# The first projection's opening: the squares' matmul placed amid the modulation row, X*rstd right behind it, one weight tile loaded first, and one later modulation pair held back

## The chip, the cores and the metric

The kernel runs on one core of a Trainium2 chip. Times are device microseconds (us), from the start of the program on the core to its end. The engines are TensorE (PE, with its weight loads shown apart as PEld), VectorE (DVE), ScalarE (ACT), GpSimd (POOL) and SyncE (SP), which here issues the DMAs. Each engine works through its own queue in order; semaphores join them.

## The reference, cut to what matters

Two transformer-like blocks follow each other on 512 tokens of width 1024, in fp32. The change touches the opening of the first one:

```python
mod = silu(c) @ w_ada + b_ada                       # 6 * 1024 values, one row
shift1, scale1, gate1, shift2, scale2, gate2 = split(mod, 6)
h = rms_norm(x, norm1_w) * (1 + scale1) + shift1    # rms_norm: x * rsqrt(mean(x*x) + eps) * w
proj = h @ w_in                                     # q, k, v, z, alpha, beta, ... of the delta rule and attention
...
qkv = silu(causal_dwconv(concat(q, k, v)))          # 4 taps; then the gated delta rule, in chunks of 64
...
x = x + gate1 * (mix @ w_o)                         # gate1, shift2, scale2, gate2 are used from here on
```

## The kernel before, in words

Activations lie transposed: 128 channels on the partitions, 512 tokens along the free axis, eight tiles k = 0 to 7 for the width of 1024. `X0` is x, `H[0]` and `H[1]` are the high and the low part of h (each weight and each activation is split in two, and `mm3` adds three matmuls, lines 314 to 316, so a projection tile of 128 outputs is 24 matmuls of 512 columns).

*The opening* (lines 395 to 481). 18 warm-up matmuls on zeros run while the first DMAs land. SP loads the vectors, x in two halves, the constants, four tiles of `w_ada1` (512 KB each), then `cb`, the row c spread over 128 partitions, and from there twelve tiles of `w_adaT` and five weight tiles in turn. The modulation is made in two ways. scale1's first half is a row on PE: `row_ps`, four tiles q with two fp32 matmuls each (two passes a matmul in the trace), which is copied to SBUF by ACT and turned into columns by the small `adcol` matmuls; with it comes `s1[:, 0:4]`. The other twelve columns (shift1, and scale1 for k of 4 and more) are products on DVE, `on_dve`: a tile of `w_adaT` times Silu of `cb`, summed along the free axis. The norm is: squares on ACT, sums on DVE (`acc`), one fp32 matmul with ones (`ss`), then Ln and Exp on ACT (`rstd`). For each k follow X*rstd on DVE, scale and shift on ACT (line 472), the split into H on ACT and DVE, and for k below 5 the load and split of one of the first five weight tiles (`first_w`, tiles 8, 9, misc, 0, 1). The first projection then is 120 matmuls over k and these five tiles.

*The delta stage* (from line 484). Stages t = 0 to 5 are lists of steps that `merge` interleaves by a position between 0 and 1: projections with their convolution (`conv_silu`: one ACT scaling out of PSUM and three DVE operations of line 560 that read the same PSUM tile, then Silu), the preparation of head pairs (`pre_steps`: E, sums, `kk`, which writes 16 small blocks to `scr` in HBM, then the substitution, which reads them back), the chain over chunks, and steps of the second modulation. For t = 0 the list has weight tiles 16 and 17; for t = 1 tile 10 is the first. Projections write into two PSUM buffers (`PSM`) from there on.

*The second modulation* (`ada_steps`, lines 331 to 352) makes 32 more columns of `mod`, which are first used after the delta stage. Its own `cb` is loaded and put through Silu when `ada_steps` is called, ahead of the lists. Each step one(j) loads four half tiles (`adraw`, two buffers) and does four products on DVE (line 344). No step of it stands in the list of t = 0; two stand in that of t = 1, at the positions 0.125 and 0.375. The projection of tile 10 is at 0.083 there, the two halves of `kk` at 0.121 and 0.170, the read back at 0.219.

*What sets the order.* The order in which lines are written is not the order in which an engine runs them. A planner goes through the program with a cost model and gives each engine, whenever it is free, the earliest written instruction whose inputs and buffers it takes to be ready. `tc.keep_in_program_order(i)` puts instruction i behind the one written before it on the same engine; what is written after i is not bound by it. ACT's functions come in table sets: `actf` (lines 248 to 267) loads the set with Ln and Exp by hand, ahead of the first of them and behind the activations of other sets that `acts` has noted in `before`; other loads are placed where a function needs them.

Of the kernel before, what the change touches and what calls it, by code (L numbers as in the profile page):

```python
# [8 lines left out]
F32 = mybir.dt.float32  # L9
F32R = mybir.dt.float32r  # L10
I32 = mybir.dt.int32
AF = mybir.ActivationFunctionType
# [3 lines left out]
P = 128  # L16
T = 512
# [195 lines left out]
def _body(ctx, tc, A):  # L213
# [20 lines left out]
    def C(name, i=0, n=None):  # L234
        o, m = CO[name]
        t = DC[0] if name in DNAMES else CS
        return t[:, o + i:o + (m if n is None else i + n)]
# [15 lines left out]
    def actf(func, **kw):  # L253
        if func not in (AF.Ln, AF.Exp):
            i = nc.scalar.activation(func=func, **kw)
            after(i, group)
            before.append(i)
            table[0] = None
            return i
        if table[0] is None:  # L260
            table[0] = tc.keep_in_program_order(nc.scalar.preload_act_table_set("natural_log_exp_and_others"))
            after(table[0], before)
            before.clear()
            group.clear()
        i = nc.scalar.activation(func=func, **kw)
        after(i, [table[0]])
        group.append(i)
        return i

    def acts(func, **kw):  # L270
        i = nc.scalar.activation(func=func, **kw)
        before.append(i)
        table[0] = None
        return i
# [23 lines left out]
    def wload(src, kt, n, own=None):  # L298
        sp = SP[0]
        if own is None:  # L300
            raw = sp.tile([P, CH], F32, tag="raw", name="raw", bufs=2)
            hi = sp.tile([P, CH], F32R, tag="hi", name="hi")
            lo = sp.tile([P, CH], F32R, tag="lo", name="lo")
        else:
            raw = own.tile([P, CH], F32, tag="ad", name="praw", bufs=15)
            hi = own.tile([P, CH], F32R, tag="phi", name="phi", bufs=len(FIRST))
            lo = own.tile([P, CH], F32R, tag="plo", name="plo", bufs=len(FIRST))
        m = kt * n
        nc.sync.dma_start(out=raw[:, :m].rearrange("p (k c) -> p k c", k=kt), in_=src)
        split(raw[:, :m], hi[:, :m], lo[:, :m])  # L310
        return (hi[:, :m].rearrange("p (k c) -> p k c", k=kt), lo[:, :m].rearrange("p (k c) -> p k c", k=kt))
# [18 lines left out]

    def ada_steps(pl):
        cb = pl.tile([P, D], F32, name="cb")
        nc.sync.dma_start(out=cb, in_=A["crow"].to_broadcast([P, D]))
        acts(func=AF.Silu, out=cb, in_=cb)

        def one(j):
            if j % 4 == 0:
                st["am"] = pl.tile([P, 4, 2], F32, tag="am", name="am", bufs=2)
            for jj in (j, j + 1):
                for q in range(2):  # L340
                    raw = pl.tile([P, T], F32, tag="adraw", name="adraw", bufs=2)
                    qs = slice(q * T, q * T + T)
                    nc.sync.dma_start(out=raw, in_=A["w_adaT"][12 + jj][:, qs])
                    nc.vector.tensor_tensor_reduce(out=raw, in0=raw, in1=cb[:, qs], scale=1.0, scalar=0.0,
                                                   op0=ALU.mult, op1=ALU.add, accum_out=st["am"][:, jj % 4, q:q + 1])
            if j % 4 == 2:
                o = mod[:, 14 + j:18 + j]
                nc.vector.tensor_tensor(out=o, in0=st["am"][:, :, 0], in1=st["am"][:, :, 1], op=ALU.add)
                nc.vector.tensor_tensor(out=o, in0=o, in1=V("b_ada", 14 + j, 4), op=ALU.add)

        st = {}
        return [lambda j=j: one(j) for j in range(0, 32, 2)]
# [42 lines left out]
    with pool("w0", 1) as w0:  # L395
# [13 lines left out]
        def ad_tile():  # L409
            return w0.tile([P, D], F32, tag="ad", name="ad", bufs=15)  # L410

        row_ps = pst.tile([P, T], F32, tag="st", name="adrow")
        for q in range(4):
            raw = ad_tile().rearrange("p (k c) -> p k c", k=2)
            nc.sync.dma_start(out=raw, in_=A["w_ada1"][q])
            for k in range(2):
                nc.tensor.matmul(row_ps[0:1], csil[:, 2 * q + k:2 * q + k + 1], raw[:, k],
                                 start=(q + k == 0), stop=(q == 3 and k == 1))
        row = w0.tile([1, T], F32, name="adrow0")
        nc.scalar.activation(out=row, in_=row_ps[0:1], func=AF.Copy)  # L420
        colp = pz.tile([P, T], F32, tag="z", name="adcol")
# [10 lines left out]
            nc.vector.tensor_tensor_reduce(out=raw, in0=raw, in1=cb, scale=1.0, scalar=0.0,  # L432
                                           op0=ALU.mult, op1=ALU.add, accum_out=am[:, m:m + 1])

        def sadd(out, a, b):
            nc.vector.tensor_tensor(out=out, in0=a, in1=b, op=ALU.add)

        acc = w0.tile([P, T], F32, name="acc0")
        for k in range(KD):
            sq = acc if k == 0 else w0.tile([P, T], F32, tag="sq", name="sq", bufs=2)  # L440
            nc.scalar.activation(out=sq, in_=X0[:, k], func=AF.Square)
            if k:
                sadd(acc, acc, sq)
        ss = ppre.tile([P, T], F32, tag="pre", name="ssx")
        nc.tensor.matmul(ss, C("ones"), acc, start=True, stop=True)
        rstd = w0.tile([P, T], F32, name="rstd")
        actf(AF.Ln, out=rstd, in_=ss, scale=1.0 / D, bias=eps)
        actf(AF.Exp, out=rstd, in_=rstd, scale=-0.5)

        W0 = {}  # L450

        def first_w(i):
            if i == "misc":
                W0[i] = wload(A["w_misc"], KD, 80, w0)
            else:
                W0[i] = wload(A["w_dn"][i], KD, P, w0)
            PS0[i] = (PSM[0] if i in FIRST[:2] else pfirst).tile([P, T], F32, tag="mm", name="mm")

        sadd(mod[:, 8:12], colp[:, 0:4], V("b_ada", 8, 4))
        nc.vector.scalar_tensor_tensor(out=s1[:, 0:4], in0=mod[:, 8:12], scalar=1.0, in1=V("norm1_w", 0, 4),  # L460
                                       op0=ALU.add, op1=ALU.mult)
        order = {0: 8, 1: 9, 2: "misc", 3: 0, 4: 1}
        for k in range(KD):
            if k >= 4:
                on_dve(4 + k, 8 + k)
                sadd(mod[:, 8 + k:9 + k], am[:, 8 + k:9 + k], V("b_ada", 8 + k))
                nc.vector.scalar_tensor_tensor(out=s1[:, k:k + 1], in0=mod[:, 8 + k:9 + k], scalar=1.0,
                                               in1=V("norm1_w", k), op0=ALU.add, op1=ALU.mult)
            on_dve(k, k)
            sadd(mod[:, k:k + 1], am[:, k:k + 1], V("b_ada", k))  # L470
            nc.vector.tensor_tensor(out=X0[:, k], in0=X0[:, k], in1=rstd, op=ALU.mult)
            nc.scalar.activation(out=X0[:, k], in_=X0[:, k], func=AF.Identity, scale=s1[:, k:k + 1],
                                 bias=mod[:, k:k + 1])
            split(X0[:, k], H[0][:, k], H[1][:, k])
            if k < len(FIRST):
                first_w(order[k])
        for k in range(KD):
            for i in FIRST:
                o = PS0[i][:80] if i == "misc" else PS0[i]
# [1297 lines left out]
```

## Time and profile before

| | |
|---|---|
| Median of three runs | 2149.95 us (2148.91 to 2151.90) |
| The profiled execution's own time | 2146.85 us |
| Its span on the core | 2145.0 us |
| Mean granted TensorE clock | 0.994 of 2.4 GHz |
| PE busy | 2112.7 us (98%) |
| DVE busy | 1209.2 us (56%) |
| ACT busy | 896.7 us (42%) |

The span runs from the first to the last instruction on the core; 1.85 us lie around it. All positions below are us from the span's start. The granted clock is 1.00 at 2.4 GHz and 0.50 at 1.2 GHz.

### The profile page before, as it was taken

How to read it: one execution, taken by the hardware profiler on the slowest of the kernel's cores; microseconds unless marked ns; L12 is line 12 of the kernel's file. 1: busy time of each engine (PE TensorE's matmuls, PEld its weight loads, DVE VectorE, ACT ScalarE, POOL GpSimd, SP SyncE). 2: the span in 40 equal slices, each digit the busy share in tenths (PEclk: the TensorE clock that was granted, in tenths of full speed). 3: DMA queues.
4: the chain of work that ended last, by engine and by line, in shares of the span. 5: the costliest groups of instructions: out<-in, count | busy, mean ns of one | idle time of the engine just before them, and what ended most of it. 6: DMA issues, size and time to landing. Idle time of an engine off the chain costs nothing.

```text
span 2145.0 us, 27476 instructions
## 1 busy us (share of the span) xinstructions
PE 2112.7 (98%) x10616; PEld 1718.3 (80%) x10616; DVE 1209.2 (56%) x2267; ACT 896.7 (42%) x1479; POOL 19.1 (1%) x50
## 2 busy tenths in 40 slices
PE   8999999999999999999999999999999999999997
PEld 5787877788888878888888887787888888888886
DVE  6776757565554554444335898555554554334446
ACT  5645433465553353333224323634443343223333
POOL 0000000000000000000000000000000000000000
PEclk9999999999999999999999999999999999999999
DMA  7443324222223343333333222133223433333332
GB/s 305 130 125 102 105 84 136 64 70 74 64 76 131 101 135 106 113 108 96 99 98 113 88 75 93 55 107 95 84 84 89 147 91 97 98 98 99 98 93 75
DMA packets 88682, 219.84 MB, mean 102 GB/s; under 512 B 23512, under 2 KB 28776, under 8 KB 87912
## 3 DMA queue, kind: packets, MB, share of 16 engines
q1 hardware_dynamic: 88552, 218.10, 32.8%
q8 instruction: 83, 1.36, 0.3%
q14 instruction: 47, 0.39, 0.1%
HBM read 211.50 MB, written 7.08 MB: 102 GB/s over the span
## 4 chain that ended last, share of the span: by engine, by line
PE 87%; DVE 6%; ACT 2%; SPq 2%; DMA 2%; issue 1%; DVEq 0%; ACTq 0%
PE mm L314 24%; PE mm L315 24%; PE mm L316 24%; PE pp L720 2%; DVE yc L1309 1%; DVE lo L296 1%; PE po L1082 1%; SPq L712 1%; PE tps L1246 1%; PE tps L1247 1%; PE tps L1248 1%; SPq L710 1%; PE ssp L602 1%; PE bpo L1638 1%; PE pw L793 1%
## 5 line engine op out<-in xcount | busy, mean ns | idle before, releaser
L295 ACT ACTIVATE hi<-raw 128x1024 fp32r<-128x1024 f32 (+4 forms) x349 | 346.6, 993 | 786.1 <-PE mm L315 671.3
L296 DVE TENSOR_TENSOR lo<-raw,hi 128x1024 fp32r<-128x1024 f32 (+4 forms) x349 | 397.9, 1141 | 453.5 <-ACT hi L295 443.8
L314 PE MATMUL mm<-H,hi 128*128 128x512 f32 x816 | 325.7, 399 | 5.5 <-DVE G L524 4.2
L316 PE MATMUL mm<-H,lo 128*128 128x512 f32 x816 | 324.3, 397 | 0.0
L315 PE MATMUL mm<-H,hi 128*128 128x512 f32 x816 | 324.2, 397 | 0.0
L314 PEld LDWEIGHTS mm<-H,hi 128*128 128x128 f32 x816 | 154.2, 189 | 39.7 <-ACT hi L295 4.6
L314 PE MATMUL mm<-XN,hi 128*128 128x512 f32 (+1 forms) x456 | 180.4, 396 | 0.0
L316 PEld LDWEIGHTS mm<-H,lo 128*128 128x128 f32 x816 | 154.2, 189 | 32.3 <-issue 3.0
L315 PEld LDWEIGHTS mm<-H,hi 128*128 128x128 f32 x816 | 154.2, 189 | 32.1 <-issue 3.2
L315 PE MATMUL mm<-XN,hi 128*128 128x512 f32 (+1 forms) x456 | 178.5, 391 | 0.0
L316 PE MATMUL mm<-XN,lo 128*128 128x512 f32 (+1 forms) x456 | 178.5, 391 | 0.0
L314 PEld LDWEIGHTS mm<-XN,hi 128*128 128x128 f32 (+1 forms) x456 | 85.0, 186 | 19.0 <-issue 1.0
L316 PEld LDWEIGHTS mm<-XN,lo 128*128 128x128 f32 (+1 forms) x456 | 84.9, 186 | 18.9 <-issue 0.8
L315 PE MATMUL mm<-HN,hi 128*128 128x512 f32 x256 | 100.1, 391 | 0.0
L314 PE MATMUL mm<-HN,hi 128*128 128x512 f32 x256 | 99.7, 389 | 0.0
L314 PE MATMUL mm<-F,hi 128*128 128x512 f32 x256 | 99.7, 389 | 0.0
L315 PE MATMUL mm<-F,hi 128*128 128x512 f32 x256 | 99.7, 389 | 0.0
L316 PE MATMUL mm<-HN,lo 128*128 128x512 f32 x256 | 99.7, 389 | 0.0
L316 PE MATMUL mm<-F,lo 128*128 128x512 f32 x256 | 99.7, 389 | 0.0
L315 PEld LDWEIGHTS mm<-XN,hi 128*128 128x128 f32 (+1 forms) x456 | 85.0, 186 | 17.6 <-issue 0.7
L1309 DVE SCALAR_TENSOR_TENSOR yc<-cp,cdh,yc 128x512 f32<-128x512 f32 x120 | 89.8, 750 | 2.9
L315 PE MATMUL mm<-FF,hi 128*128 128x512 f32 x176 | 68.5, 389 | 0.0
(676 smaller groups left out, 3887.4 us busy)
## 6 DMA issues: line engine op xcount, KB each, us to landing
raw<-in_w_ff SPq DMA_DIRECT2D x64, 512.0 KB, 3.6
raw<-in_ffn_up SPq DMA_DIRECT2D x44, 512.0 KB, 3.5
adraw<-in_w_adaT SPq DMA_DIRECT2D x64, 256.0 KB, 3.2
raw<-in_w_ga SPq DMA_DIRECT2D x32, 512.0 KB, 3.5
raw<-in_w_dn SPq DMA_DIRECT2D x28, 512.0 KB, 3.9
raw<-in_w_br SPq DMA_DIRECT2D x32, 256.0 KB, 2.7
raw<-in_ffn_down SPq DMA_DIRECT2D x16, 448.0 KB, 3.4
ad<-in_w_adaT SPq DMA_DIRECT2D x12, 512.0 KB, 10.2
```

Of the source, the lines that this page charges most:

```text
L295: nc.scalar.activation(out=hi, in_=src, func=AF.Copy)
L296: nc.vector.tensor_tensor(out=lo, in0=src, in1=hi.bitcast(F32), op=ALU.subtract)
L314: nc.tensor.matmul(ps, wh, xh, start=start, stop=False)
L315: nc.tensor.matmul(ps, wh, xl, start=False, stop=False)
L316: nc.tensor.matmul(ps, wl, xh, start=False, stop=stop)
L602: nc.tensor.matmul(ssp[64 * h:64 * h + 64, kind * 8 + c:kind * 8 + c + 1], sq[:, c], C("ones", 0, 1), start=True, stop=True)
L710: nc.sync.dma_start(out=U[r0:r0 + 16, :, r0:r0 + 16], in_=scr[1, q0:q0 + 4].rearrange("c j i -> j c i"))
L712: nc.sync.dma_start(out=Xb[r0:r0 + 16, :, r0:r0 + 16], in_=scr[2, q0:q0 + 4].rearrange("c j i -> j c i"))
L720: nc.tensor.matmul(pp[:, c4], lh[:, c4], rh[:, c4], start=True, stop=True)
L793: nc.tensor.matmul(pw[64 * h:64 * h + 64], st["wt"][b][:, c4, 64 * h:64 * h + 64], S[:, h], start=True, stop=True)
L1082: nc.tensor.matmul(po[:, qs], VT[:, kb, hh], pT[:, kb * P:kb * P + P], start=(kb == 0), stop=(kb == qb))
L1309: i = nc.vector.scalar_tensor_tensor(out=ycs[m], in0=cps[m][:, s:s + T], scalar=cdh[:, m * 31 + s:m * 31 + s + 1], in1=ycs[m], op0=ALU.mul ...
```

## The change

In `ada_steps`, the load of `cb` and its Silu move into the first step, one(0), and that load and the half tiles of the first column (jj = 0) are pinned behind what is written before them on SP. In the opening, squares, sums and `first_w` are written ahead of the modulation row, and the first weight tile (8) is loaded there; the `ss` matmul is pinned behind the row's second tile (q = 1), and Ln, Exp and all eight X*rstd are written right behind it. The loop over k loads the other four weight tiles, each one step of k earlier than before.

```diff
@@ -330,17 +330,20 @@
 
     def ada_steps(pl):
         cb = pl.tile([P, D], F32, name="cb")
-        nc.sync.dma_start(out=cb, in_=A["crow"].to_broadcast([P, D]))
-        acts(func=AF.Silu, out=cb, in_=cb)
 
         def one(j):
+            if j == 0:
+                tc.keep_in_program_order(nc.sync.dma_start(out=cb, in_=A["crow"].to_broadcast([P, D])))
+                acts(func=AF.Silu, out=cb, in_=cb)
             if j % 4 == 0:
                 st["am"] = pl.tile([P, 4, 2], F32, tag="am", name="am", bufs=2)
             for jj in (j, j + 1):
                 for q in range(2):
                     raw = pl.tile([P, T], F32, tag="adraw", name="adraw", bufs=2)
                     qs = slice(q * T, q * T + T)
-                    nc.sync.dma_start(out=raw, in_=A["w_adaT"][12 + jj][:, qs])
+                    i = nc.sync.dma_start(out=raw, in_=A["w_adaT"][12 + jj][:, qs])
+                    if jj == 0:
+                        tc.keep_in_program_order(i)
                     nc.vector.tensor_tensor_reduce(out=raw, in0=raw, in1=cb[:, qs], scale=1.0, scalar=0.0,
                                                    op0=ALU.mult, op1=ALU.add, accum_out=st["am"][:, jj % 4, q:q + 1])
             if j % 4 == 2:
@@ -409,6 +412,26 @@
         def ad_tile():
             return w0.tile([P, D], F32, tag="ad", name="ad", bufs=15)
 
+        def sadd(out, a, b):
+            nc.vector.tensor_tensor(out=out, in0=a, in1=b, op=ALU.add)
+
+        acc = w0.tile([P, T], F32, name="acc0")
+        for k in range(KD):
+            sq = acc if k == 0 else w0.tile([P, T], F32, tag="sq", name="sq", bufs=2)
+            nc.scalar.activation(out=sq, in_=X0[:, k], func=AF.Square)
+            if k:
+                sadd(acc, acc, sq)
+        W0 = {}
+
+        def first_w(i):
+            if i == "misc":
+                W0[i] = wload(A["w_misc"], KD, 80, w0)
+            else:
+                W0[i] = wload(A["w_dn"][i], KD, P, w0)
+            PS0[i] = (PSM[0] if i in FIRST[:2] else pfirst).tile([P, T], F32, tag="mm", name="mm")
+
+        order = {0: 8, 1: 9, 2: "misc", 3: 0, 4: 1}
+        first_w(order[0])
         row_ps = pst.tile([P, T], F32, tag="st", name="adrow")
         for q in range(4):
             raw = ad_tile().rearrange("p (k c) -> p k c", k=2)
@@ -416,6 +439,15 @@
             for k in range(2):
                 nc.tensor.matmul(row_ps[0:1], csil[:, 2 * q + k:2 * q + k + 1], raw[:, k],
                                  start=(q + k == 0), stop=(q == 3 and k == 1))
+            if q == 1:
+                ss = ppre.tile([P, T], F32, tag="pre", name="ssx")
+                tc.keep_in_program_order(nc.tensor.matmul(ss, C("ones"), acc, start=True, stop=True))
+                rstd = w0.tile([P, T], F32, name="rstd")
+                actf(AF.Ln, out=rstd, in_=ss, scale=1.0 / D, bias=eps)
+                actf(AF.Exp, out=rstd, in_=rstd, scale=-0.5)
+        
+                for k in range(KD):
+                    nc.vector.tensor_tensor(out=X0[:, k], in0=X0[:, k], in1=rstd, op=ALU.mult)
         row = w0.tile([1, T], F32, name="adrow0")
         nc.scalar.activation(out=row, in_=row_ps[0:1], func=AF.Copy)
         colp = pz.tile([P, T], F32, tag="z", name="adcol")
@@ -432,34 +464,9 @@
             nc.vector.tensor_tensor_reduce(out=raw, in0=raw, in1=cb, scale=1.0, scalar=0.0,
                                            op0=ALU.mult, op1=ALU.add, accum_out=am[:, m:m + 1])
 
-        def sadd(out, a, b):
-            nc.vector.tensor_tensor(out=out, in0=a, in1=b, op=ALU.add)
-
-        acc = w0.tile([P, T], F32, name="acc0")
-        for k in range(KD):
-            sq = acc if k == 0 else w0.tile([P, T], F32, tag="sq", name="sq", bufs=2)
-            nc.scalar.activation(out=sq, in_=X0[:, k], func=AF.Square)
-            if k:
-                sadd(acc, acc, sq)
-        ss = ppre.tile([P, T], F32, tag="pre", name="ssx")
-        nc.tensor.matmul(ss, C("ones"), acc, start=True, stop=True)
-        rstd = w0.tile([P, T], F32, name="rstd")
-        actf(AF.Ln, out=rstd, in_=ss, scale=1.0 / D, bias=eps)
-        actf(AF.Exp, out=rstd, in_=rstd, scale=-0.5)
-
-        W0 = {}
-
-        def first_w(i):
-            if i == "misc":
-                W0[i] = wload(A["w_misc"], KD, 80, w0)
-            else:
-                W0[i] = wload(A["w_dn"][i], KD, P, w0)
-            PS0[i] = (PSM[0] if i in FIRST[:2] else pfirst).tile([P, T], F32, tag="mm", name="mm")
-
         sadd(mod[:, 8:12], colp[:, 0:4], V("b_ada", 8, 4))
         nc.vector.scalar_tensor_tensor(out=s1[:, 0:4], in0=mod[:, 8:12], scalar=1.0, in1=V("norm1_w", 0, 4),
                                        op0=ALU.add, op1=ALU.mult)
-        order = {0: 8, 1: 9, 2: "misc", 3: 0, 4: 1}
         for k in range(KD):
             if k >= 4:
                 on_dve(4 + k, 8 + k)
@@ -468,12 +475,11 @@
                                                in1=V("norm1_w", k), op0=ALU.add, op1=ALU.mult)
             on_dve(k, k)
             sadd(mod[:, k:k + 1], am[:, k:k + 1], V("b_ada", k))
-            nc.vector.tensor_tensor(out=X0[:, k], in0=X0[:, k], in1=rstd, op=ALU.mult)
             nc.scalar.activation(out=X0[:, k], in_=X0[:, k], func=AF.Identity, scale=s1[:, k:k + 1],
                                  bias=mod[:, k:k + 1])
             split(X0[:, k], H[0][:, k], H[1][:, k])
-            if k < len(FIRST):
-                first_w(order[k])
+            if k < 4:
+                first_w(order[k + 1])
         for k in range(KD):
             for i in FIRST:
                 o = PS0[i][:80] if i == "misc" else PS0[i]
```

## Rows read from the trace of the kernel before

**Rows 1.** The page, whole span: busy us, share and instructions of each engine.
```profile
PE 2112.7 (98%) x10616; PEld 1718.3 (80%) x10616; DVE 1209.2 (56%) x2267; ACT 896.7 (42%) x1479; POOL 19.1 (1%) x50
```

**Rows 2.** Windows by stage: us, busy (instructions) per engine, PEclk, DMA share, GB/s.
```profile
0.00:56.15 56.15, 46.35 (x165) 30.36 (x165) 38.61 (x74) 30.70 (x42) 6.13 (x16) 0.94 0.78 303
56.15:83.00 26.85, 22.63 (x125) 18.26 (x125) 21.53 (x45) 20.03 (x31) 0.00 (x0) 0.87 0.39 115
...
104.00:160.00 56.00, 56.00 (x315) 46.30 (x312) 44.72 (x121) 26.14 (x44) 0.00 (x0) 1.00 0.40 120
```

**Rows 3.** Waits of PE from 56 to 160 us: total us, times, longest.
```profile
PE mm L314 <- DVE G L524: 4.2, 1, 4.2
```

**Rows 4.** Windows, as rows 2: granted clock (PEclk) in short stretches.
```profile
9.00:10.00 1.00, 0.00 (x0) 0.00 (x0) 0.79 (x3) 0.77 (x2) 0.00 (x0) 1.00 1.01 414
23.50:24.00 0.50, 0.00 (x0) 0.00 (x0) 0.50 (x2) 0.50 (x2) 0.00 (x0) 0.50 1.06 426
71.50:72.00 0.50, 0.00 (x0) 0.00 (x0) 0.44 (x3) 0.50 (x2) 0.00 (x0) 0.50 0.67 242
78.00:79.00 1.00, 1.00 (x6) 0.83 (x5) 0.36 (x2) 1.00 (x2) 0.00 (x0) 0.98 0.24 29
```

**Rows 5.** Timeline of PE, 0 to 26 us: start, us, instruction, idle before.
```profile
1.42 6.70 PE L405 MATMUL zero<-wz 128*128 128x512 f32 x18 [1.42 <-POOL wz L402]
10.63 7.03 PE L417 MATMUL adrow<-ad,csil 128*1 128x512 f32 x16 [2.51 <-ACT sq L441]
17.59 1.13 PE L445 MATMUL ssx<-acc,CS 128*128 128x512 f32 x2
18.80 1.05 PE L423 MATMUL adcol<-CS,adrow 1*128 1x1 f32 x8
25.26 0.79 PE L314 MATMUL mm<-H,phi 128*128 128x512 f32 x1 [5.42 <-ACT H L295]
```

**Rows 6.** Timeline of DVE, 63 to 73 us.
```profile
63.20 0.75 DVE L560 SCALAR_TENSOR_TENSOR cacc<-mm,VS,cacc 128x511 f32<-128x511 f32 x1 [0.54 <-ACT cacc L558]
63.87 0.68 DVE L344 CUSTOM_DVE_ANT_0 adraw<-adraw,cb 128x512 f32<-128x512 f32 x1
...
70.29 1.21 DVE L296 TENSOR_TENSOR lo<-raw,hi 128x1024 fp32r<-128x1024 f32 x1
...
71.68 0.74 DVE L560 SCALAR_TENSOR_TENSOR cacc<-mm,VS,cacc 128x509 f32<-128x509 f32 x1
```

**Rows 7.** Timeline of ACT, 14 to 62 us.
```profile
15.79 1.06 ACT L271 ACTIVATE cb<-cb 128x1024 f32<-128x1024 f32 x1 [3.71 <-DMA cb<-in_crow]
16.87 1.28 ACT L261 ACT_TABLE_LOAD   x1
18.16 0.59 ACT L420 ACTIVATE adrow<-adrow 1x512 f32<-1x512 f32 x1
...
19.60 0.66 ACT L265 ACTIVATE rstd<-ssx,CS 128x512 f32<-128x512 f32 x1
...
60.86 1.06 ACT L271 ACTIVATE cb<-cb 128x1024 f32<-128x1024 f32 x1
```

**Rows 8.** Timeline of SP's queue, 100 to 116 us.
```profile
102.27 8.12 SPq L653 DMA_DIRECT2D scr<-C  x16
```

**Rows 9.** Windows of the instructions on adraw alone, columns as rows 2.
```profile
56.00:104.00 48.00, 8.08 (x12) 0.93 0.44 131
```

**Rows 10.** Timeline of SP's queue, 9 to 13 us.
```profile
10.51 0.33 SPq L309 DMA_DIRECT2D praw<-in_w_dn  x1
11.79 0.33 SPq L431 DMA_DIRECT2D ad<-in_w_adaT  x1
```

**Rows 11.** Timeline of DVE, 7 to 24 us.
```profile
7.54 5.47 DVE L436 TENSOR_TENSOR acc<-acc,sq 128x512 f32<-128x512 f32 x7 [7.54 <-ACT sq L441]
17.14 1.23 DVE L432 CUSTOM_DVE_ANT_0 ad<-ad,cb 128x1024 f32<-128x1024 f32 x1 [4.13 <-DMA ad<-in_w_adaT]
...
22.45 0.69 DVE L471 TENSOR_TENSOR X<-X,rstd 128x512 f32<-128x512 f32 x1
```

## The prediction

> **What bounds the kernel now.** I read the page first: TensorE (PE) is busy in 98% of the span [rows 1], so time can only go where PE stands still or runs at half clock. The table by stages shows where that is. The stage up to 56.15 us, the first projection, has PE busy 46.35 of 56.15 us; the stage from 56.15 to 83 has 22.63 of 26.85 us at a mean granted clock of 0.87; from 104 to 160 PE is busy all the time at full clock [rows 2]. The list of PE's waits from 56 to 160 us is headed by one of 4.2 us, ahead of a projection matmul [rows 3]. The clock rows say what such a gap costs behind itself. The granted clock is 1.00 in the 2.5 us gap between the warm-up matmuls and the modulation row, but it is down at 0.50 (1.2 GHz) at 23.5 us, in the gap of 5.4 us before the first projection, and at 71.5 us, in the 4.2 us gap; that second time it is back (2.4 GHz) at 78 us [rows 4, 5].
>
> Two chains lie ahead of these gaps. The first projection waits for H of k = 0, that is for rstd, X*rstd, s1 and mod. The gap at 68 to 72.6 us ends when a PSUM buffer comes free: there are two, and the new weight pair's first matmul needs the one that the convolution of w_dn 16 reads. The third and last read (L560) runs on DVE from 71.68 to 72.42 us, and PE starts at 72.57. DVE has no idle time to speak of from 63.20 on, and in between stand three products of the second modulation (L344) and one `lo` split of 1.21 us [rows 6]. Ahead of 63.20, ACT spends 1.06 us on that modulation's Silu of `cb` [rows 7].
>
> **The held pair.** `cb` of the second modulation is no longer loaded ahead of everything. Its DMA is now pinned behind what is written before it on SP. In the merged list of stage t = 1 the step one(0) stands at 0.125 and the first half of kk at 0.121, so the DMA follows eight of the sixteen `scr` writes, which before start at 102.27 us [rows 8]. All products need `cb`, the unpinned ones too, so all 12 products that ran between 56 and 104 us (8.08 us of DVE [rows 9]) leave that stretch, not the two pinned loads alone.
>
> What this takes from the chain to 72.57: the Silu, 1.06 us on ACT, and three products at 0.6 us net each (0.68 long, the next operation starts 0.6 later [rows 6]), 1.8 us. A fourth, before 63.20, stood in a wait for ACT and is free. Together 2.9 us, and 4.0 if the planner also puts the `lo` split behind the reads. PE's gap shrinks from 4.2 to 1.3 us or less. A gap of 2.5 us left the clock at 1.00 [rows 4, 5], so I expect no drop: from 72.57 to 78.0 us PE did at half clock what takes half of 5.4 us, and 2.7 us come back. Sum: 2.9 + 2.7 = 5.6 us gained; bounds 5.6 and 6.7.
>
> The Trainium skill ("TensorE: Matmul & The Clock Gate", Loop structure matters more than you think) has matmuls go cold when the loop waits between them, while evacuation beside dense matmuls does not cost the clock. The rows agree at 4.2 us (0.50) and show that 2.5 us can pass. [...]
>
> **Where the 12 products go.** Behind 104 us. DVE is busy 44.72 of the 56 us up to 160 [rows 2], so 8.08 us more make 52.8: they fit, but hardly beside the substitution, whose small dependent operations also run on DVE there. Against that, the steps before it lose their own products and start earlier by what PE gained. On SP three issues of about 0.4 us come between the two halves of the `scr` writes (sixteen in 8.12 us [rows 8]), ahead of the load that the substitution waits for: 1.2 us later. PE has projection matmuls to fill with: it is busy for all of 104 to 160 us [rows 2]. I cost this at 0.5 us; bounds 0 and 8.1 (all twelve on the chain).
>
> **The first projection.** Moving one weight tile (512 KB) to the front of the queue moves every tile behind it by one place, up to the place of the fifth weight tile (the other four each come one step of k earlier): the queue takes one such tile each 1.28 us (10.51 to 11.79 [rows 10]). So the modulation row starts at 10.63 + 1.28 = 11.9 us. Its 16 passes are about 0.43 us apart (7.03 us over 16 [rows 5]); behind eight of them, at 15.3, the squares' matmul can run (the sums, ready at 13.0, are early enough [rows 11]; 1.13 us [rows 5]), then Ln and Exp at 0.66 each [rows 7]: rstd stands at 17.8 us and not at 20.9, 3.1 us earlier. Eight X*rstd at about 0.6 follow on DVE, to 22.7.
>
> That is no gain of 3.1 us. H of k = 0 also needs s1 and mod 0. The row's second half now ends 1.3 us late for the tile and 0.9 us for the squares' matmul, at about 19.8; the row's copy (0.59 [rows 7], behind ACT's Silu at 20.2), the column matmuls (1.05 [rows 5]) and two small DVE operations put s1 near 22.3. For mod 0, `cb` must go through Silu: it lands at 15.79 + 1.28 = 17.1, but ACT now does Ln and Exp first, then loads Silu's table (1.28 [rows 7]) and is through at 20.2. The product of k = 0 (1.22 us [rows 11]) starts at 20.2 if the planner takes it at once, or at 22.7 if it puts all eight earlier written X*rstd first; before it started at 17.14. So H's last input is there at 22.3 (s1) or about 24.1 (mod 0). Add the 2.1 us that lay between the end of X*rstd of k = 0 and the first matmul (23.14 to 25.26 [rows 5, 11]), less what the larger part of it, ACT's queue, may save: PE starts at about 24.0 or 26.2, before at 25.26. If it starts at 24.0 the clock may hold as well. The stage's mean of 0.94 over 56.15 us [rows 2] is 6.7 us at 0.50, from 23.5 to 30.2; 5 us of them lie behind PE's start, so this is worth up to 2.5 us. Bounds: 3.8 us gained and 0.9 lost. DVE does the same work in the stretch with an idle hole filled, and PE eats what it delivers. I take 0: the early half and the late half are about as likely.
>
> The moved split of the first weight tile, on ACT and DVE, falls where both wait for DMA (ACT 3.71 us ahead of `cb`'s Silu, DVE 4.13 us ahead of the first product [rows 7, 11]) and costs nothing. Were that cover gone it would cost about 1.2 us on each ahead of rstd.
>
> The Trainium skill ("ScalarE: Activation LUTs", Table sets: the hidden batching unit) speaks against this part: one set's functions should all be done before a switch. Before, both Silus of this stage ran ahead of Ln; now Ln and Exp part them, which is one load more. The trace has a load at 1.28 us, and the sum above holds it.
>
> **Sum.** 5.6 gained, 0 at the front, 0.5 given back: 5.1 us. The profiled execution's own time is 2146.85 us, so 2141.7 by that; the median of the three runs shown is 2149.95, and 2144.8 by that, which is my number. 0.2% of it, about what can be told from no change, is 4.3 us.
>
> **Rivals.**
> *The front gains too* (chance 0.09): product 0 early and the clock held, 3 us of the 3.8: 2141.8.
> *The modulation row runs at half clock* (0.19): PE's gap ahead of it grows from 2.5 to 3.8 us, between the one that kept the clock and those in which it was down 3.1 us in (68.35 to 71.5) and 3.6 us in (19.85 to 23.5) [rows 3 to 5]. The eight passes ahead of the squares then take 6.8 us and not 3.4, rstd is 3.4 us later and so is H: 2148.2. For it: the gap's length; against it: both clocks fell in gaps that were longer in the end (4.2 and 5.4 us).
> *Part is given back* (0.14): the held products, once `cb` lands, go ahead of the new pair's reads, and another PSUM wait appears near 105 to 130 us, 4.2 us with its 2.7 us behind it, less the 0.5 already counted: about 2151.
> *Slower* (0.12): the substitution chain becomes the bound. All twelve products on it are 8.1 us, the SP issues 1.2, and PE's idle time loses the clock again, 2.7: 12.0 us against 5.6 gained, 2156.4. It decides the sign once more than 9.9 us come back. For it: DVE at 80% there, and small operations that any 0.68 us product pushes back. Against it: the chain's beginning moves earlier by the same products' absence.
>
> **How the numbers follow.** The forecast itself has 0.46, with a range of its own of 2142.3 to 2147.5; of the 0.46, 0.39 lies beyond 4.3 us. Faster: 0.39 + 0.09 = 0.48. Same: 0.07 + 0.19 + 0.14 = 0.40. Slower: 0.12. The range goes from the front's gain, 2141.0, to the part given back, 2151.5, and leaves out the slower case and the ends.
>
> **What would show it.** Right: no PE wait over 1.5 us between 60 and 80 us, granted clock 1.00 there; no L344 before about 95 us; `cb`'s second DMA among the `scr` writes; the squares' matmul between two halves of the row; rstd near 18 us; the first projection's last matmul within 1 us of 56.15. Wrong: granted clock 0.50 in the row; a new PE wait near 105 to 160; the gap at 68 us still there because another operation, not the products, holds the PSUM buffer.

## The result and the profile after

The changed kernel takes 2162.19 us, median of 5 runs (2160.28 to 2169.01); the kernel before, run beside it, 2151.31 (5 runs). The ratio is 1.0065 (95% interval 1.0053 to 1.0077): some 14 us slower (10.9 us by the medians). The forecast, 2144.8 us with 2151.5 as its upper end, was wrong, and on the side to which it gave 0.12. The profiled execution's own time is 2162.19, its span 2160.4 us, 15.4 more than before.

The table by stages of the kernel after (columns as in [rows 2]):

```profile
0.00:56.15 56.15, 41.17 (x139) 26.35 (x140) 39.46 (x74) 33.03 (x42) 6.20 (x16) 0.88 0.76 293
56.15:83.00 26.85, 26.60 (x153) 20.85 (x151) 16.42 (x29) 19.43 (x31) 0.00 (x0) 1.00 0.11 38
83.00:104.00 21.00, 21.00 (x126) 16.58 (x126) 10.69 (x28) 11.50 (x17) 0.00 (x0) 0.84 0.20 56
104.00:160.00 56.00, 54.74 (x298) 44.24 (x297) 48.09 (x134) 27.10 (x45) 0.00 (x0) 0.97 0.57 173
...
220.00:260.00 40.00, 35.11 (x174) 27.20 (x175) 26.66 (x87) 14.74 (x29) 0.53 (x1) 0.91 0.35 102
...
290.00:310.00 20.00, 20.00 (x105) 14.14 (x104) 10.49 (x41) 5.94 (x17) 0.00 (x0) 0.74 0.04 5
```

Three windows of the kernel before that the prediction did not look at:

```profile
83.00:104.00 21.00, 20.44 (x151) 16.39 (x149) 14.95 (x47) 13.05 (x21) 0.00 (x0) 1.00 0.49 150
...
220.00:260.00 40.00, 39.22 (x258) 31.70 (x258) 26.10 (x68) 16.59 (x38) 1.57 (x3) 1.00 0.39 111
...
290.00:310.00 20.00, 19.93 (x95) 15.86 (x93) 16.62 (x68) 5.78 (x11) 0.00 (x0) 1.00 0.31 89
```

Read them against [rows 2] as standing time plus busy time lost to the clock. The stage that the hold was to mend is mended: 26.60 us busy at 1.00, where it was 22.63 at 0.87. The first projection is worse: 41.17 busy for 46.35. And four stretches behind it, at full clock before, are not any more: 83 to 104 (0.84), 104 to 160 (1.3 us of standing and 0.97), 220 to 260 (4.9 us of standing and 0.91), 290 to 310 (0.74, with no standing at all).

ACT at the front of the kernel after, 12 to 22 us:

```profile
13.04 1.28 ACT L261 ACT_TABLE_LOAD   x1
14.32 1.28 ACT L271 ACT_TABLE_LOAD   x1
16.98 1.06 ACT L271 ACTIVATE cb<-cb 128x1024 f32<-128x1024 f32 x1 [1.37 <-DMA cb<-in_crow]
18.05 1.28 ACT L265 ACT_TABLE_LOAD   x1
19.34 0.69 ACT L265 ACTIVATE rstd<-ssx,CS 128x512 f32<-128x512 f32 x1
20.09 0.59 ACT L452 ACTIVATE adrow<-adrow 1x512 f32<-1x512 f32 x1
20.70 1.28 ACT L265 ACT_TABLE_LOAD   x1
21.99 0.63 ACT L265 ACTIVATE rstd<-rstd 128x512 f32<-128x512 f32 x1
```

PE and, behind it, DVE in the same place:

```profile
11.88 3.59 PE L440 MATMUL adrow<-ad,csil 128*1 128x512 f32 x8 [3.64 <-DMA ad<-in_w_ada]
15.41 1.13 PE L444 MATMUL ssx<-acc,CS 128*128 128x512 f32 x2
...
20.73 1.05 PE L455 MATMUL adcol<-CS,adrow 1*128 1x1 f32 x8 [0.68 <-ACT adrow L452]
30.96 1.57 PE L314 MATMUL mm<-H,phi 128*80 128x512 f32 x3 [9.19 <-ACT H L295]
```

```profile
22.66 4.91 DVE L450 TENSOR_TENSOR X<-X,rstd 128x512 f32<-128x512 f32 x8 [0.59 <-ACT rstd L265]
27.48 0.15 DVE L416 TENSOR_TENSOR mod<-adcol,VS 128x4 f32<-128x4 f32 x1
...
28.68 0.15 DVE L468 SCALAR_TENSOR_TENSOR s<-mod,VS 128x4 f32<-128x4 f32 x1
```

The squares' sum stands at 16.5 us. But ACT, which was idle, had loaded the Ln/Exp table, then Silu's table for `cb`, and has to load the other again: Ln begins at 19.34, a fourth load follows, and Exp ends at 22.6. Then eight X*rstd, 4.91 us, run ahead of the two small operations that make s1, whose column was ready at 21.8, and a weight split of 1.22 us runs between the two. PE starts 5.7 us later than before.

SP's queue behind 104 us, kernel after:

```profile
105.74 3.72 SPq L659 DMA_DIRECT2D scr<-C  x8
109.50 0.42 SPq L336 DMA_DIRECT2D cb<-in_crow  x1
109.97 0.91 SPq L344 DMA_DIRECT2D adraw<-in_w_adaT  x2
110.98 3.80 SPq L659 DMA_DIRECT2D scr<-C  x7
117.80 0.97 SPq L344 DMA_DIRECT2D adraw<-in_w_adaT  x2
118.81 0.43 SPq L659 DMA_DIRECT2D scr<-C  x1
...
121.90 0.53 SPq L687 DMA_DIRECT2D BK<-scr  x1
```

ACT in the same place, and SP's queue before:

```profile
115.98 1.06 ACT L271 ACTIVATE cb<-cb 128x1024 f32<-128x1024 f32 x1
```

```profile
112.12 0.53 SPq L681 DMA_DIRECT2D BK<-scr  x1
```

There are two adraw buffers. The second pair of weight loads waits for the first product (117.07 us on DVE), and that for Silu of `cb`, which ACT takes up at 115.98 us, 6.5 us after the row was issued; the sixteenth `scr` write and the load of BK, on which the substitution depends, stand behind it. BK is issued at 121.90 us; before, at 112.12.

### The profile page after: what moved, and what is told of

Same layout as the page of the kernel before. It is cut to its first block, busy times and chain, and to the rows that moved or that the text cites. A ratio compares the mean times of both kernels' runs of the same rounds, so it can differ in the third digit from the quotient of the medians.

```text
span 2160.4 us, 27482 instructions
## 1 busy us (share of the span) xinstructions
PE 2122.8 (98%) x10616; PEld 1722.8 (80%) x10616; DVE 1213.2 (56%) x2267; ACT 900.9 (42%) x1481; POOL 19.3 (1%) x50
## 4 chain that ended last, share of the span: by engine, by line
PE 90%; DVE 5%; ACT 2%; DMA 1%; issue 1%; SPq 1%; DVEq 0%; ACTq 0%
PE mm L315 25%; PE mm L314 25%; PE mm L316 25%; PE pp L726 2%; DVE yc L1315 1%; DVE lo L296 1%; PE po L1088 1%; PE tps L1252 1%; PE tps L1253 1%; PE tps L1254 1%; PE ssp L608 1%; PE bpo L1644 1%; PE pw L799 1%; PE pc L826 1%; PE ss L816 1%
```

## The experiments

All ratios are to the kernel before, run beside each, with 95% intervals; 0.001 is 2.1 us.

**Each part alone, and the hold without SP's queue.** The front alone (e1) is the changed kernel with `ada_steps` of before:

```diff
     def ada_steps(pl):
         cb = pl.tile([P, D], F32, name="cb")
+        nc.sync.dma_start(out=cb, in_=A["crow"].to_broadcast([P, D]))
+        acts(func=AF.Silu, out=cb, in_=cb)
...
-                    if jj == 0:
-                        tc.keep_in_program_order(i)
```

The hold alone (e2) is the kernel before with `ada_steps` of the changed one. In e3, which is e2 but for this, BKI holds the first load of BK and the steps stand behind it in the merged list:

```diff
-                tc.keep_in_program_order(nc.sync.dma_start(out=cb, in_=A["crow"].to_broadcast([P, D])))
+                after(nc.sync.dma_start(out=cb, in_=A["crow"].to_broadcast([P, D])), BKI[:1])
...
-                        tc.keep_in_program_order(i)
+                        after(i, BKI[:1])
```

> The front part alone; the modulation steps stand as in the kernel before. Theory A (two losses that add): the first projection starts near 31 us instead of 25.26, as in the changed kernel, and the 5 to 7 us stay to the end: 2156 to 2159 us, with the products of the later modulation again at 56 to 104 us and the load of BK at about 118 (5.7 later than the 112.12 of before). Theory B (the late front upsets the order behind 104 us): BK and the substitution are late by more than 10 us here too, and the whole of the 14 us appears: 2163 to 2167 us.

> The held pair alone; the front is that of before. Theory A: first projection at 25.3, PE gains 5.6 to 7 us by 80 us, then the load of BK stands behind the held pair in SP's queue, the substitution starts 4 to 10 us later than in the kernel before, and the stage behind 104 us gives back 12 to 18 us: 2156 to 2161 us. Theory B: without the late front nothing is given back but the forecast 0.5 us: 2145 to 2147 us.

> The held pair alone, but the broadcast row and the pair's weights are issued behind the load of BK, so that no block write and no load of BK stands behind them in SP's queue. Theory A1 (the loss behind 104 us is SP's queue): BK is issued 5 to 7 us earlier than 112.12, the gain at 80 us stays: 2144 to 2148 us. Rival A2 (the loss is the 12 products themselves on VectorE among the substitutions, or matmuls at the half clock): 8 us or more come back although BK is on time: 2153 to 2160 us.

Front alone: 1.0029 (1.0018 to 1.0040), +6 us, its first projection at 30.89 us. Hold alone: 1.0060 (1.0047 to 1.0073), +13. Behind BK: 1.0013 (1.0005 to 1.0022), +3. Windows of the hold alone:

```profile
56.15:83.00 26.85, 25.29 (x173) 19.86 (x171) 17.52 (x31) 22.07 (x35) 0.00 (x0) 1.00 0.12 40
83.00:104.00 21.00, 21.00 (x113) 16.44 (x112) 14.45 (x35) 11.14 (x18) 0.00 (x0) 0.84 0.31 85
...
220.00:260.00 40.00, 35.04 (x184) 28.03 (x183) 26.58 (x88) 14.17 (x28) 1.05 (x2) 0.91 0.43 125
290.00:310.00 20.00, 20.00 (x87) 14.05 (x86) 7.52 (x34) 3.83 (x12) 0.00 (x0) 0.57 0.00 1
```

and of the hold behind BK:

```profile
104.00:160.00 56.00, 51.21 (x292) 41.14 (x290) 40.10 (x116) 25.12 (x44) 0.52 (x1) 1.00 0.44 131
220.00:260.00 40.00, 40.00 (x278) 33.01 (x277) 27.73 (x74) 17.88 (x41) 1.57 (x3) 1.00 0.31 91
290.00:310.00 20.00, 20.00 (x136) 16.66 (x136) 11.89 (x45) 8.04 (x10) 0.00 (x0) 1.00 0.27 67
```

BK's load in the hold alone and, in e3, ahead of the pair:

```profile
118.79 0.53 SPq L684 DMA_DIRECT2D BK<-scr  x1
```

```profile
110.92 0.52 SPq L686 DMA_DIRECT2D BK<-scr  x1
```

In the hold alone BK is issued at 118.79 us and the losses at 230 and 300 us are there without the changed front; with BK at 110.92 both are gone. Theory B is out, and the queue carries some 10 of 13 us. The substitution does not get longer by the held products: from its first step to its end it takes 24.1 us in the hold alone, with 11 products among its steps, 24.3 behind BK, with 10, and 25.9 before, with 8. It only starts later. But the gain did not stay either: 4.8 us of standing came in at 104 to 160, most of it waits for DVE.

What counts is lateness against TensorE's own work. With the front alone BK is issued at 118.98 us, as late as in the hold alone, but the block writes ahead of it are late by as much (108.94 us against 102.27 before), and at 220 to 260 and 290 to 310 us that kernel runs as the one before.

**A late substitution without any hold.** In e5, the kernel before but for this, BK of the first pair is loaded six times into one tile:

```diff
-            nc.sync.dma_start(out=st["BK"], in_=A["scr"][p][0])
+            for _ in range(6 if p == 0 else 1):
+                nc.sync.dma_start(out=st["BK"], in_=A["scr"][p][0])
```

> The kernel before with nothing held, but for the first pair BK is loaded six times into the same tile, each load behind the landing of the one before, so that the substitution starts some 8 to 12 us later than at 116.36 us. It does no other work. Theory A1 (a late substitution is what costs the time behind 104 us, whatever makes it late): idle and half-clock stretches of TensorE appear at 220 to 310 us as in the changed kernel, 7 to 15 us are lost: 2156 to 2164 us. Rival A2 (TensorE has other work and the late load alone is covered; the cost comes from the products on VectorE): 2151 us or less.

1.0046 (1.0033 to 1.0059), +10 us (7 by the medians). The last load is issued at 127.69, 15.6 us later than BK before, and the losses stand in the same places, smaller:

```profile
220.00:260.00 40.00, 36.93 (x218) 29.71 (x217) 26.96 (x83) 15.45 (x33) 1.05 (x2) 0.96 0.33 100
290.00:310.00 20.00, 19.86 (x92) 14.67 (x92) 16.80 (x67) 5.26 (x11) 0.00 (x0) 0.92 0.28 87
```

The substitution's last operation before, in the hold alone and here:

```profile
142.21 0.37 DVE L697 COPY XK<-UK 64x256 f32<-64x256 f32 x1
```

```profile
147.28 0.38 DVE L700 COPY XK<-UK 64x256 f32<-64x256 f32 x1
```

```profile
148.12 0.37 DVE L698 COPY XK<-UK 64x256 f32<-64x256 f32 x1
```

Lateness alone does it; none of the twelve products has left its place at 56 to 104 us in this kernel. The end of the substitution, not the issue of BK, says how late the chain is: it is 5.9 us late here and 5.1 in the hold alone.

**The hold elsewhere.** In e6 row and Silu are early again and only the pair is held; in e7 the steps follow the load of w_dn-3 (from e2):

```diff
     def ada_steps(pl):
         cb = pl.tile([P, D], F32, name="cb")
+        nc.sync.dma_start(out=cb, in_=A["crow"].to_broadcast([P, D]))
+        acts(func=AF.Silu, out=cb, in_=cb)
```

```diff
-        merge((0, 0.9, ch), (0, 0.68, pr), (0.7, 1, l0), (0.04, 0.27, late), pj, (0, 0.5, ad), (0, 0.6, g0))
+        merge((0, 0.9, ch), (0, 0.68, pr), (0.7, 1, l0), (0.04, 0.27, late), pj, (0.585, 0.75, ad) if t == 1 else (0, 0.5, ad), (0, 0.6, g0))
```

In e11 row and pair follow the first `scr` write of XK, as in e3 they follow BK, and NADA, the number of steps in each stretch t, goes from (0, 2, 2, 2, 4, 6) to (0, 0, 3, 3, 4, 6). e8 and e12 are e7 and e11 with the mended front e4 (below); e16 is e12 with (0, 0, 2, 2, 2, 10), e15 with (0, 0, 0, 0, 4, 12), row and first column behind the fourth `scr` write of XK and the first load of every later step pinned. In e15 that hold did not take: no fourth write stood in the program yet where the first step is written, so the row went out at 55.76 us and the first pair's four products ran at 61.70 to 69.93, much as before; the loads of the other 60 came from 318 us on.

> The held pair alone, but the broadcast row and its Silu are where they stood before (row at 51 us, Silu at 61), so a held weight tile waits for no Silu and its buffer comes free as soon as its product has run. Theory A1 in its narrower form (what holds up SP is the wait for a buffer that the late Silu keeps full): BK is issued near 112 us and the time is that of the kernel with the pair behind BK, 2148 to 2152 us. If the place of the pair amid the block writes costs by itself, BK is at 116 us or later and the time 2156 us or more.

> The held pair alone, held for less long: row and weights are issued behind the load of the weight tile w_dn-3 (near 72 us) and ahead of the block writes, so the products start near 78 us. The three products that stood ahead of w_dn-10's evictions at 64 to 70 us are gone from there, the sixteen block writes and BK are not held up. If both readings are right (the gain is those three products, the loss is SP's queue): TensorE gains 4 to 7 us by 83 us, BK comes at 108 to 113 us and the time is 2142 to 2147 us. If what was gained comes back by itself behind 83 us, as 7 of the 5 to 7 us did with the pair behind BK: 2148 to 2152 us.

> The short hold together with the front that has the Silu behind Ln and Exp and each X*rstd in the loop. That front alone measured no change, so the sum is that of the short hold: 2142 to 2147 us; if the two shift each other's order, up to 2152 us.

> The later modulation held until the substitution of the first pair is written back (its twelve steps then fall on the stages behind), front of before: no product stands amid the first substitution, and nothing of the modulation stands ahead of BK in SP's queue. If the loss behind 104 us is the substitution's late end (start of BK plus products among its steps), it ends at 130 to 136 us instead of 142.2, the pairs behind it run as early as TensorE lets them, and the 5 to 7 us gained by 83 us stay: 2139 to 2146 us. If TensorE's gain can't be kept because the products only collide further on (second pair, end of the stage at 432 us): 2149 to 2158 us.

> The same hold with the front that has Silu behind Ln and Exp and X*rstd in the loop: the time of the hold behind the substitution, changed by -2 to +2 us, since that front alone measured no change.

> The front with Silu behind Ln and Exp and X*rstd in the loop, and all sixteen steps of the later modulation behind the third pair's work, each step's first load kept at its place in the program: the products fall on the last pair's substitution and on the end of the stage. Theory C: the chain of the pairs runs 5 to 10 us ahead up to 330 us, and what the 64 products cost comes back at 340 to 460 us: 2142 to 2155 us, faster than before only if the last pair's chain bears them.

> The same front, the hold behind the first write-back, and the steps dealt out as 2, 2, 2 and 10 over the third to the sixth stretch. By theory C the last pair gets fewer products than with 3, 3, 4 and 6: 2145 to 2150 us; if the planner fills free buffers as before, no change from that kernel, 2149 to 2152 us.

Row and Silu early (e6): 1.0039 (1.0027 to 1.0052). BK is issued at 114.82, so the late Silu was 4 us of its delay, but the time is 8 us above before: my narrower theory fell. On DVE products stood ahead of and between the substitution's first steps (at 118.37 and 119.73 us), and it lasted 27.3 us and ended at 146.3. Short hold: 1.0066 (1.0052 to 1.0080), with the front 1.0048 (1.0032 to 1.0065), where I expected a gain. BK came early (110.69), but this order has the substitution last from 115.2 to 146.1 us, 30.9 in place of 25.9, and TensorE meets a wait that no other order above had:

```profile
PE mm L314 <- ACT qrr L994: 4.5, 1, 4.5
```

It ends at 445.8 us, at the entry to the next stage, with half clock around it. Behind the substitution: 1.0025 (1.0015 to 1.0035), with the front 1.0014 (1.0003 to 1.0025). In the latter the substitution ended at 132.2 and not 142.2 us, but the last pair's transposes ran at 433.85, 1.9 us later than before: ten us of lead were gone by the end. Spread later: 1.0024 (1.0014 to 1.0034), with a wait of 6.8 us for OAs at 443; 60 of the products pinned later still: 1.0161 (1.0147 to 1.0175), with one wait of 30.6 us for DVE up to 461. No place beat the kernel before.

**What any placing could give.** In e14 all 64 products, their loads, row and Silu are left out of the kernel before, in e13 the first twelve of e11 (the same edit for j < 6), so these parts of the later modulation are not computed:

```diff
-            for jj in (j, j + 1):
+            nc.gpsimd.memset(st["am"][:, j % 4:j % 4 + 2], 0.0)
+            for jj in ():
```

> As the hold behind the first substitution with the front of before, but the twelve products and their weight loads that the kernel before ran at 56 to 104 us are left out altogether, so that parts of the later modulation are not computed; the other 52 run behind the first write-back. Theory C (the products only change their place: moved behind 104 us they cost VectorE's chain there what they cost TensorE at 72 us): without the twelve the gain of 5 to 7 us stays, 2141 to 2146 us. Rival D (the early gain is lost in any case, since the chain of the pairs does not start earlier): 2148 us or more.

> The kernel before with all 64 products of the later modulation, their row, Silu and weight loads left out, so that this modulation is not computed. It bounds what any placing of them can give. Theory C: they cost the stage at 56 to 432 us 8 to 20 us: 2129 to 2141 us. Rival D (they are covered wherever they stand and the losses come from the order of the queues): within 5 us of before, 2143 us or more.

Without twelve: 0.9993 (0.9984 to 1.0001), no change that can be told; 2147.43 us lies between what theory C and rival D had. Without all: 0.9975 (0.9964 to 0.9985), -5.4 us. Its substitution's end and its last transposes, and the last transposes before:

```profile
130.38 0.37 DVE L695 COPY XK<-UK 64x256 f32<-64x256 f32 x1
```

```profile
410.94 0.63 PE L833 MATMUL tpo<-CS,o 128*128 128x128 f32 x4
```

```profile
431.95 0.63 PE L835 MATMUL tpo<-CS,o 128*128 128x128 f32 x4
```

The write-back is 12 us earlier than before, the end of the pairs 21 us, and what is won is, by its size, the gap at 72 us and the half clock behind it. Theory C's 8 to 20 us are refuted; rival D holds in so far as TensorE itself is the bound from 104 us on (busy for all but 1.1 of the 356 us up to 460).

**The front, mended.** From e1, e9 orders Silu of `cb` behind Ln and Exp, e10 puts each X*rstd into the loop again, and e4 does both:

```diff
-        acts(func=AF.Silu, out=cb, in_=cb)
+        after(acts(func=AF.Silu, out=cb, in_=cb), group)
```

```diff
-                for k in range(KD):
-                    nc.vector.tensor_tensor(out=X0[:, k], in0=X0[:, k], in1=rstd, op=ALU.mult)
...
             sadd(mod[:, k:k + 1], am[:, k:k + 1], V("b_ada", k))
+            nc.vector.tensor_tensor(out=X0[:, k], in0=X0[:, k], in1=rstd, op=ALU.mult)
```

> The front alone with one effect taken out: the Silu of the broadcast row is ordered behind Ln and Exp; the eight X*rstd stay together. If the order of the activation tables is the larger cost, Exp ends at 17.5 to 18 us where the modulation row runs at full clock (about 20.5 where it runs at half), the eight X*rstd end near 22.5 and hide behind the row copy and the columns, the first projection starts near 25 to 27 us: 2147 to 2151 us. If the eight products ahead of s1 are the larger cost, it starts at 28.5 us or later: 2153 us or more.

> The front alone with the other effect taken out: each X*rstd in the loop again, the Silu still ahead of Ln. If the table order is the larger cost, Exp still ends at 22 us or later and the first projection starts at 27 us or later: 2151 to 2155 us. If the eight products are, it starts near 26 us: 2147 to 2151 us.

> The front alone with two of its effects taken out: the Silu of the broadcast row is ordered behind the Ln and Exp, and each X*rstd stands in the loop again. If the two extra table loads and the eight X*rstd ahead of s1 are what cost the 5.7 us, rstd is ready near 18 us instead of 22.6 and the first projection starts at 23.5 to 26 us: 2149 to 2152 us. Rival (the late first weights or the late modulation row cost it): the first projection starts at 28 us or later and the time stays at 2154 us or more.

Silu behind: 1.0012 (1.0001 to 1.0023); X in the loop: 1.0006 (0.9996 to 1.0017); both: 1.0000 (0.9987 to 1.0012). Either mend takes off most of the 6 us, both take all; which of the two is worth more the intervals don't tell. The first matmuls came at 28.65, 27.20 and 27.49 us, later than expected, and in these executions the modulation row lost the clock: its first eight passes took 5.29, 5.29 and 6.27 us, in place of 3.59. PE with both:

```profile
11.78 6.27 PE L437 MATMUL adrow<-ad,csil 128*1 128x512 f32 x8 [3.40 <-DMA ad<-in_w_ada]
...
19.04 3.59 PE L437 MATMUL adrow<-ad,csil 128*1 128x512 f32 x8
27.49 1.14 PE L314 MATMUL mm<-H,phi 128*80 128x512 f32 x2 [3.05 <-ACT H L295]
```

**The changed kernel mended.** The edit of e3 inside the changed kernel (e17), and with it those of e9 and e10 (e18):

> The changed kernel with one thing mended: row and pair are issued behind the load of BK. If the two losses stand for themselves, what is left is the front's 6 us and the hold's 1 to 3 us: 2154 to 2158 us, and the stretches at 230 to 240 and 290 to 300 us run at the full clock. If the late front alone is enough to make the chain of the pairs late: 2159 us or more.

> The changed kernel with all three mended: pair behind BK, Silu behind Ln and Exp, each X*rstd in the loop. By the sum of the single runs (+1 to +5 us for the hold behind BK, -3 to +3 for that front): 2147 to 2154 us, so no change from the kernel before; if the two fit together better than apart, 2144 us or less.

Hold mended: 1.0050 (1.0035 to 1.0066); all: 1.0011 (1.0002 to 1.0020). So 14 us become 11 and then 2. The stretches at 230 and 290 us are whole again in the first, as expected, but the time is above the expected 2154 to 2158 (2158.96): its profiled execution, 2155.22 us long, had the row at half clock (6.50 us for eight passes) and the first projection at 33.7 us. All three kernels with the hold behind BK (e3, e17, e18) stand for 4.9 us between 104 and 220 us, the kernel before for 0.5: that is nearly what the hold gains ahead of it. What a mend saves seems to hang on the order in which one mends: BK is 10 us of the hold alone and 3 of the changed kernel with its late front, where the intervals before and after that mend overlap. The three causes account together for all but 2 us; a price for each inside the 14 the runs don't give.

## Why the prediction was wrong

*The held pair: right.* Forecast 5.6 us (2.9 of gap, 2.7 of clock). In the hold alone the stage [rows 2] loses 1.56 us of standing and nothing to the clock; before, it lost 4.2 us and half of the 5.4 us at half clock: 5.4 us less. Leaving all products out gave 5.4 us in time. Of the gap of 4.2 us [rows 3] 2.7 were these products; 1.6 stay in the hold alone, and as much without any product. (That row names DVE's G, L524, as the release, and not the read that I named; G runs right behind it, at 72.34 to 72.52 us, behind the same products.) Part of this was luck. That a gap of 2.5 us leaves the clock at 1.00 I had read from one execution; in others the modulation row lost it behind a gap of 1.9 to 2.1 us (below). The 1.6 us left here kept it.

*Where the 12 products go: the step that failed.* I put 0.5 us there, between 0 and 8.1, and costed three issues ahead of BK at 1.2 us. I had seen which instructions stand in front of the `scr` writes and not what they wait for: two buffers, so the third load waits for a product, and that for the Silu of a row just issued. BK was 9.8 us late in the changed kernel, 6.7 in the hold alone. From the first block write to BK it took 16.2 us and 16.9, before 9.9 and with the front alone 10.0, so 6 to 7 us are the queue's in both kernels, and the rest in the changed one is its late front. The second error is the cover: "PE has projection matmuls to fill with" holds at 104 to 160 us, where little is lost, but the late pair comes back at 230 us (4.9 us standing, 3.6 of them waits for DVE at the output transposes, and half clock) and near 290 to 300 us. My slower rival had the right place, the substitution chain, but for the most part the wrong agent, DVE's products: with BK on time and the same twelve products behind 104 us the cost was 3 us, and with the substitution late and no product moved it was 7 to 10. Products ahead of and among the substitution's steps seem to cost too: in e6 and e7 (8 and 14 us) it lasted 27.3 and 30.9 us; how much of those is theirs stays open.

*The front: the sum failed, 0 against 6.* Two of its steps were wrong. "ACT now does Ln and Exp first": the planner put the Silu first, which it could, since the helper for Silu is ordered only behind what it needs; that it took the row to be there earlier is a guess, for in the trace the row landed at 16.98 us and the squares' sum stood at 16.54. So ACT waited 1.37 us for the row with Ln's input ready for the last 0.4 of it, and rstd came at 22.6 and not 17.8. "Two small DVE operations put s1 near 22.3": they ran behind eight products, at 28.7. I had allowed for the eight ahead of mod 0 but not ahead of s1. The rival that I gave 0.19, the modulation row at half clock, has no part in the 5.7 us of the changed kernel's trace: there, and with the front alone, the first eight passes took 3.59 us. In the 9 other traces with this front they took 5.2 to 6.5 us behind gaps of 3.15 to 4.64 us. But the front of before has this too. In five of its nine traces the 16 passes took 8.7 us and not 7.03, behind gaps of 1.91 to 3.38 us, as in the hold alone; in the other four, behind gaps of 2.36 to 3.00 us, they kept the clock:

```profile
10.43 8.67 PE L420 MATMUL adrow<-ad,csil 128*1 128x512 f32 x16 [2.05 <-ACT sq L444]
```

So the length of the gap does not tell these executions apart, and my argument for this rival from its length does not hold. The page that I quoted against this part, the Trainium skill ("ScalarE: Activation LUTs", Table sets: the hidden batching unit), has one set's functions done before a switch. The trace agrees: with the Silu behind Exp two of the four loads, 1.28 us each, are gone.

*Right in detail:* the row at 11.9 us, the squares' matmul at 15.4, no product ahead of 104 us, `cb` between two halves of the block writes.

## What to carry to other kernels

Ahead of an in-order DMA queue, ask of each load that a change puts there what frees its buffer: if that is work which a load just ahead of it starts, everything behind it waits for the whole round trip. A part that takes idle time from the bound engine has a ceiling that can be measured by leaving the work out (5.4 us here), and what lateness on a chain without slack costs does not stop there (13 us in the hold alone); price the second before the first. Where a planner orders an engine, an operation that should come second must be made to, or the planner decides, table loads included: here it put first the one whose input landed later.

## What the runs showed of the hardware

The clock fell where TensorE did not stand still. Without the 64 products, behind a stretch from 78.9 us in which 64 one-column matmuls (ssp) stand among the others:

```profile
82.00:84.00 2.00, 2.00 (x22) 1.40 (x20) 0.57 (x1) 2.00 (x4) 0.00 (x0) 1.00 0.03 8
84.00:90.00 6.00, 6.00 (x26) 5.11 (x27) 4.35 (x11) 0.83 (x1) 0.00 (x0) 0.50 0.12 13
```

It did the same in the hold alone, behind BK and in the changed kernel, 3.4 us each, so part of the hold's gain was lost at once; with the hold behind the substitution and the mended front the same matmuls kept 1.00, as they did before. It is no mark of the hold: 13 of the 20 traces have a granted clock of 0.76 to 0.92 at 83 to 104 us, those of the front alone and of the mended front among them. What decides it is not settled. Likewise, ahead of the modulation row, a gap of 3.64 us kept the clock in one execution and one of 1.91 lost it in another.
